# Half the key tiles of an attention stream stored as differences and accumulated onto a used score bank

## The chip, the core and the metric

One core of a Trainium2 chip. The metric is device time in microseconds (us), the median of several executions of one program, lower is better. The engines are TensorE (PE; its weight loads are PEld), VectorE (DVE), ScalarE (ACT), GpSimd (POOL) and the queues that issue DMAs, SyncE's (SP) above all.

## The reference

One layer over 4096 tokens of width 1024 with 16 learned tokens ahead of them (4112 positions). After an RMS norm, one projection feeds two branches:

```python
# Fourier branch: 8 groups of 64 channels, 2-D DFT over positions and channels
fr = jnp.real(jnp.fft.fftn(f, axes=(1, 3), norm='ortho'))
out = jnp.einsum('blgc,gcd->blgd', fr, w_fmix) + b_fmix          # times silu(gate)
# attention branch: 8 query heads, 2 key/value heads of 64, normed and rotated q and k
s = jnp.einsum('bkgqd,bksd->bkgqs', q_blk, k) * (HEAD_DIM ** -0.5)
p = jax.nn.softmax(s, axis=-1)
out = jnp.einsum('bkgqs,bksd->bkgqd', p, v)                      # times silu(gate)
# both: output projection, residual, final RMS norm, the 16 tokens dropped
```

## The kernel before

Everything is computed nearly to float32: an operand is split into a high part in float16 and a low part that holds the rest, and a product is the sum of high x high, low x high and high x low.

**Projection stage** (`phase_a`, to about 700 us). It goes through 33 tiles of 128 positions (tile `NT` = 32 holds the 16 learned tokens) in the order of the list `order`. For each tile TensorE projects to keys and values, queries and two gates (`proj`, in five PSUM banks), VectorE and POOL rotate and norm, `tile_stack` splits queries and keys and `tile_tr` writes them to DRAM (`q_d`, `k_d`); values go to `v_d`. A list of slots (`at`, `deal`) hangs the work of the Fourier branch between the tiles: folds on POOL (`fold_scale`, `fold_lo`), VectorE and ScalarE, and their matmuls (`fproj`).

A key tile is kept as two 128x128 matrices `K[kv][:, 0]` and `K[kv][:, 1]`, written by DMA transposes (`k_load`, `k1_load`). The first has the high part of the keys in rows 0 to 63 and again in 64 to 127; the second has the low part in rows 0 to 63 and the constant 256 in rows 64 to 71. A query block `qA` has high and low parts above each other; `qB` the high part and, in rows 64 to 71, the row maxima times -1/256. So two full matmuls of 512 columns give a score less its bound:

```python
T.matmul(s, K[kv][:, 0, t * P:(t + 1) * P], qa, start=True, stop=False)
T.matmul(s, K[kv][:, 1, t * P:(t + 1) * P], qb, start=False, stop=True)
```

**Stream** (`phase_b`, from about 780 us). 8 query blocks of 512 by 4 pairs of heads make 32 pairs. A pair is 66 steps, 33 key tiles for each of two heads. A step (`step`) has:

- the two score matmuls into one of two banks `s` (pool `pq`);
- `pe`, the exp on ScalarE;
- `rr`, the residual `pe` less its upper half, on POOL or VectorE (VectorE at 16 of the 66);
- five steps later (`LAG = 5`, list `pend`) nine value matmuls into the bank `o` (`pvm`), four query groups of 128 columns. At a head's end ScalarE copies `o` to `tt`, and VectorE and POOL divide and gate.

A bound on each query's scores is needed before its pair. For it 16 **maxima runs** stand in the pair before (list `AT`): a run is two groups (`grp`) of two half-array matmuls, one head in rows 0 to 63 and one in rows 64 to 127 (queries `qP`, copied by DMA), high parts alone, each group into a tile of two banks (pool `pm`, two tiles). VectorE reduces each group over 1024 scores. `red`, `fin` and `put` at steps 61, 63 and 64 turn the maxima into the rows of `qB`; `meta` does the 16 learned tokens. A true maximum is not needed, only a bound that is near enough.

The output projection of the block before (`out_units`, 48 matmuls of 512 columns a pair, at steps 15 to 62 from the fifth pair on) and its norm (`NORM`, `square`, `newton`) are dealt to fixed steps. In the first four pairs (`block0`) the Fourier branch's matmuls stand there instead, two or three a step (`f_step`), with transposes and mixes (`trans`, `mix`) that use `pm` too. Ahead of the first pair its maxima alternate with 11 Fourier matmuls each. After the last pair the last block is projected.

Program order is the order on each engine; the waits come from the tiles.

Of the kernel before, what the change touches and what calls it, by code (L numbers as in the profile page):

```python
# [32 lines left out]
P = 128  # L33
# [5 lines left out]
NT = 32  # L39
# [90 lines left out]
def phase_a(tc, a, pool, mm3, id16, id32, sc):  # L130
# [15 lines left out]
    pos = {t: j for j, t in enumerate(order)}  # L146
    with ExitStack() as st:
# [18 lines left out]
        ksb = [wp.tile([P, 2, 2, 2, HD], F16, name=f"ks{i}") for i in range(3)]  # L166
# [157 lines left out]
        def tile_kv(t):  # L324
# [16 lines left out]
            store(v_d[t, :n], vst[:n])  # L341
# [29 lines left out]

        def tile_stack(t):

            n, qn, ks = xs[t][0], live[t]["t1"], ksb[pos[t] % 3]
            kn = qn[:n, 8 - live[t]["o"]:]
# [4 lines left out]
            S.activation(ks[:n, :, 0, 0], kn, AF.Copy)  # L380
            S.activation(ks[:n, :, 0, 1], kn, AF.Copy)
            V.tensor_tensor(out=ks[:n, :, 1, 0], in0=kn, in1=ks[:n, :, 0, 0], op=ALU.subtract)

        def tile_tr(t):
            n, ks = xs.pop(t)[0], ksb[pos[t] % 3]
            z = live.pop(t)
            store(k_d[t * P:t * P + n], ks[:n].rearrange("p a w b c->p (a w b c)"))
# [220 lines left out]
        def runs(ts):  # L608
            out = [(t, t + 1) for t in ts if t == NT]
            for t in sorted(ts):  # L610
                if t < NT:
                    if out and out[-1][1] == t:
                        out[-1] = (out[-1][0], t + 1)
                    else:
                        out.append((t, t + 1))
            return out

        at(done * 4 + 2 - 3 * 4, ld["k_load"], runs(order[:done]))
        ld["rest"] = runs(order[done:])
# [10 lines left out]
        for t in ksb:  # L630
            G.memset(t, 0.0)
            G.memset(t[:, :, 1, 1, 0:8], 256.0)
# [107 lines left out]
def phase_b(tc, a, pool, mm3, id32, id16, sc):  # L740
# [10 lines left out]
    with ExitStack() as st:  # L751
# [5 lines left out]
        pm = pool(st, "pm", 2, PSUM)  # L757
        pq = pool(st, "pq", 2, PSUM)
        pv = pool(st, "pv", 1, PSUM)
        pp = pool(st, "po", 1, PSUM)  # L760
        K = [ld["kk"][0], bp.tile([P, 2, (NT + 1) * P], F16, name="K1")]
# [3 lines left out]
        qP = [bp.tile([P, 4, QB], F16, name=f"qP{i}") for i in range(2)]  # L765
# [25 lines left out]
        def v_load(i):  # L791
            if i == 3:
# [87 lines left out]
        def trans(u, early):  # L880
# [3 lines left out]
            else:  # L884
                ps = pm.tile([P, 2, 512], F32, tag="m", name="m")[:, 0].rearrange("p (g c)->p g c", c=P)
# [40 lines left out]
        def mix(u, early):  # L926
            n = 64 if seq[u] is LAST else P
            mo = mos[:, 2 * (u % 2):2 * (u % 2) + 2]
            if early:
                t = [pq.tile([P, 512], F32, tag="s", name="s") for _ in range(2)]  # L930
            else:
                t = pm.tile([P, 2, 512], F32, tag="m", name="m")
                t = [t[:, i] for i in range(2)]
# [86 lines left out]

        met, rowt = {}, []

        def max_units(i):
            b, p = pairs[i]
            kv, q, n = p // 2, qP[b % 2], nm[i % 2]
            mx = sm.tile([P, 4, 2, 8], F32, tag="mx", name="mx")

            def grp(s, c):
                t = pm.tile([P, 2, 512], F32, tag="m", name="m")
                for e in range(2):  # L1030
                    rs = slice(64 * e, 64 * e + 64)
                    T.matmul(t[:, e], q[rs, p, s * P:(s + 1) * P], K[kv][rs, 0, c * 512:(c + 1) * 512],  # L1032
                             start=True, stop=True)
                V.tensor_reduce(mx[:, s, :, c], t, axis=AX.X, op=ALU.max)  # L1034

            def meta():
# [4 lines left out]
                t = pm.tile([P, 2, 512], F32, tag="m", name="m")  # L1041
                for x in ps:
                    for e in range(2):
                        rs = slice(64 * e, 64 * e + 64)
                        for s in range(4):
                            o = 64 * x + 16 * s
                            T.matmul(t[:, e, o:o + 16], q[rs, x, s * P:(s + 1) * P], K[x // 2][rs, 0, NTOK:L],
                                     start=x == ps[0] and s == 0, stop=True, skip_group_check=x > ps[0] or s > 0)
                mb = met[b][:, :, ps[0]:ps[-1] + 1]
                V.tensor_reduce(mb, t[:, :, 64 * ps[0]:64 * ps[-1] + 64].rearrange("p e (x s k)->p e x s k", s=4, k=16),  # L1050
                                axis=AX.X, op=ALU.max)
                V.tensor_scalar(out=mb, in0=mb, scalar1=-1.0 / 256.0, scalar2=None, op0=ALU.mult)

            def red():
                m = sm.tile([P, 4, 2], F32, tag="mm", name="mm")
                V.tensor_reduce(m, mx, axis=AX.X, op=ALU.max)
                V.scalar_tensor_tensor(out=n[:, 64:72].rearrange("p (e s)->p e s", s=4),
# [3 lines left out]
            def fin():  # L1061

                t = pm.tile([P, 2, 512], F32, tag="m", name="m")
                T.matmul(t[:, 0, :P], n, id16, start=True, stop=True)
                rowt.append(t)

            def put():
                t = rowt.pop()
                V.tensor_tensor(  # L1069
                    out=qB[b % 2].rearrange("p (q e) (s c)->p e s q c", e=2, c=P)[64:72, :, :, p],  # L1070
                    in0=t[64:72, 0, :P].unsqueeze(1).unsqueeze(1).broadcast_to([8, 2, 4, P]),
                    in1=id32[64:72, 64:72].rearrange("p (e s)->p e s", s=4).unsqueeze(3).broadcast_to([8, 2, 4, P]),
# [503 lines left out]
```

## Time and profile before

| | |
|---|---|
| time, median of 3 executions | 3203.95 us (3200.87 to 3204.02) |
| the profiled execution | 3203.48 us, span 3201.7 us |
| mean granted TensorE clock | 0.995 |
| busy: TensorE / VectorE / POOL / ScalarE | 98% / 74% / 72% / 52% |

The span is the time from the first to the last instruction of the profile. A busy share is that of the time in which at least one instruction of the engine ran. TensorE's matmuls overlap, so that the mean duration of one is longer than the time from its start to the start of the next. A row of the costliest groups reads: line, engine, operation, output and inputs, form and count, then busy us and mean ns of one, then how long the engine stood idle just before these instructions, and what ended most of that.

### The profile page before, as it was taken

How to read it: one execution, taken by the hardware profiler on the slowest of the kernel's cores; microseconds unless marked ns; L12 is line 12 of the kernel's file. 1: busy time of each engine (PE TensorE's matmuls, PEld its weight loads, DVE VectorE, ACT ScalarE, POOL GpSimd, SP SyncE). 2: the span in 40 equal slices, each digit the busy share in tenths (PEclk: the TensorE clock that was granted, in tenths of full speed). 3: DMA queues.
4: the chain of work that ended last, by engine and by line, in shares of the span. 5: the costliest groups of instructions: out<-in, count | busy, mean ns of one | idle time of the engine just before them, and what ended most of it. 6: DMA issues, size and time to landing. Idle time of an engine off the chain costs nothing.

```text
span 3201.7 us, 77151 instructions
## 1 busy us (share of the span) xinstructions
PE 3146.1 (98%) x32291; PEld 1831.4 (57%) x32291; DVE 2373.2 (74%) x3241; ACT 1667.2 (52%) x2965; POOL 2304.3 (72%) x2174
## 2 busy tenths in 40 slices
PE   8999999998999999999999999999999999999998
PEld 4555555545666655555555555555555555555554
DVE  6666566647677778878888778788887887788774
ACT  5433333324555555555555555555555555555563
POOL 5655565536777788877877888887787778888762
PEclk9999999999999999999999999999999999999999
DMA  7444544648422221012111211201120111111112
GB/s 243 146 161 147 152 156 153 182 155 228 131 68 86 78 61 31 28 28 64 28 28 38 54 28 31 58 28 28 38 54 28 35 41 43 31 31 28 28 49 68
DMA packets 238832, 247.67 MB, mean 77 GB/s; under 512 B 134658, under 2 KB 182658, under 8 KB 235538
## 3 DMA queue, kind: packets, MB, share of 16 engines
q1 hardware_dynamic: 224658, 217.57, 23.6%
q10 hardware_dynamic: 13824, 25.17, 2.1%
q8 instruction: 252, 4.13, 0.5%
q14 instruction: 98, 0.80, 0.1%
HBM read 139.59 MB, written 66.38 MB: 64 GB/s over the span
## 4 chain that ended last, share of the span: by engine, by line
PE 74%; DVE 1%; ACT 0%; DMA 0%; issue 0%; POOL 0%; SPq 0%; ACTq 0%; DVEq 0%; POOLq 0%
PE s L1102 14%; PE s L1101 14%; PE o L1122 13%; PE po L1197 9%; PE m L1032 8%; PE o L1129 8%; PE o L1127 2%; PE o L1125 2%; PE pd L849 2%; PE m L1389 1%; DMA acs<-acs_d 0%; ACT pe L1105 0%; POOL rr L1107 0%; DVE rr L1107 0%; DVE thl L893 0%
## 5 line engine op out<-in xcount | busy, mean ns | idle before, releaser
L1107 POOL TENSOR_TENSOR rr<-pe 128x512 f16<-128x512 f32 x1572 | 1709.9, 1105 | 469.9 <-ACT pe L1105 463.4
L1105 ACT ACTIVATE pe<-s 128x512 f32<-128x512 f32 x2112 | 1259.5, 597 | 1016.1 <-PE s L1102 903.2
L1034 DVE TENSOR_REDUCE mx<-m 128x2 f32<-128x1024 f32 x1024 | 1205.9, 1220 | 180.7 <-PE m L1032 179.2
L1129 PE MATMUL o<-VV,rr 128*128 128x65 f16 x8448 | 975.7, 193 | 0.2 <-POOL rr L1107 0.2
L1129 PEld LDWEIGHTS <-rr 128*128 128x128 f16 x8448 | 784.5, 98 | 175.6 <-POOL rr L1107 7.4
L1122 PE MATMUL o<-VV,pe 128*128 128x129 f16 x6336 | 843.3, 222 | 0.8 <-ACT tt L1133 0.8
L1102 PE MATMUL s<-qB,K 128*128 128x512 f16 x2112 | 800.3, 379 | 1.4 <-DVE qB L1069 1.4
L1101 PE MATMUL s<-qA,K 128*128 128x512 f16 x2112 | 799.6, 379 | 0.7 <-ACT pe L1105 0.7
L1122 PEld LDWEIGHTS <-pe 128*128 128x128 bf16 x6336 | 591.1, 97 | 365.1 <-issue 191.0
L1107 DVE TENSOR_TENSOR rr<-pe 128x512 f16<-128x512 f32 x540 | 453.4, 840 | 213.8 <-ACT pe L1105 207.1
L1125 PE MATMUL o<-VV,pe 128*128 128x65 f16 x2112 | 411.5, 195 | 0.0
L1127 PE MATMUL o<-VV,pe 128*128 128x64 f16 x2112 | 410.6, 194 | 0.0
L303 PE MATMUL ps<-wh,xh 128*128 128x512 f16 (+2 forms) x1032 | 352.7, 354 | 9.5 <-ACT xh L291 9.0
L304 PE MATMUL ps<-wl,xh 128*128 128x512 f16 (+2 forms) x1032 | 352.6, 354 | 2.5 <-DVE wl L274 2.5
L1032 PE MATMUL m<-K,qP 64*128 64x512 f16 x2048 | 313.7, 382 | 9.6 <-DMA qP<-qA 6.0
L306 PE MATMUL ps<-wh,xl 128*128 128x512 f16 x768 | 291.6, 380 | 0.0
L1127 PEld LDWEIGHTS <-pe 128*128 128x128 bf16 x2112 | 209.2, 99 | 0.0
L1125 PEld LDWEIGHTS <-pe 128*128 128x128 bf16 x2112 | 206.5, 98 | 0.0
L1102 PEld LDWEIGHTS <-K 128*128 128x128 f16 x2112 | 205.1, 97 | 1.7 <-issue 1.6
L1101 PEld LDWEIGHTS <-K 128*128 128x128 f16 x2112 | 203.4, 96 | 0.9 <-issue 0.4
L1032 PEld LDWEIGHTS <-qP 64*128 64x128 f16 x2048 | 59.7, 94 | 229.2 <-issue 221.3
L1197 PE MATMUL po<-woh,mt 128*128 128x512 f16 x448 | 169.8, 379 | 1.0 <-DVE hh L1202 1.0
(209 smaller groups left out, 3429.2 us busy)
## 6 DMA issues: line engine op xcount, KB each, us to landing
room<-x SPq DMA_DIRECT2D x32, 512.0 KB
xt<-xt SPq DMA_DIRECT2D x32, 512.0 KB
sg<-fx SPq DMA_DIRECT2D x16, 1024.0 KB
xr<-x SPq DMA_DIRECT2D x32, 512.0 KB
out<-yo SPq DMA_DIRECT2D x32, 512.0 KB
ct<-cdo SPq DMA_DIRECT2D x9, 1088.0 KB
fg_d<-g ACTq DMA_DIRECT2D x32, 256.0 KB
ag_d<-g ACTq DMA_DIRECT2D x32, 256.0 KB
```

The costliest lines, as they stand in the source:

```text
L303: T.matmul(o, xh[:, d, :n], wh[:, d, c0:c1], start=d == 0, stop=False)
L1032: T.matmul(t[:, e], q[rs, p, s * P:(s + 1) * P], K[kv][rs, 0, c * 512:(c + 1) * 512], start=True, stop=True)
L1034: V.tensor_reduce(mx[:, s, :, c], t, axis=AX.X, op=ALU.max)
L1101: T.matmul(s, K[kv][:, 0, t * P:(t + 1) * P], qa, start=True, stop=False)
L1102: T.matmul(s, K[kv][:, 1, t * P:(t + 1) * P], qb, start=False, stop=True)
L1105: S.activation(pe, s, AF.Exp, scale=HD ** -0.5)
L1107: eng.tensor_tensor(out=rr, in0=pe, in1=hi, op=ALU.subtract)
L1122: T.matmul(o[:, c0:c0 + 129], hi[:, cs], va, start=t == 0 and s == 0, stop=t == NT, skip_group_check=True)
L1125: T.matmul(o[:, c0:c0 + 65], hi[:, cs], vh, start=False, stop=t == NT, skip_group_check=True)
L1127: T.matmul(o[:, c0:c0 + 64], hi[:, cs], vl, start=False, stop=t == NT, skip_group_check=True)
L1129: T.matmul(o[:, c0:c0 + 65], rr[:, cs], vh, start=False, stop=t == NT, skip_group_check=True)
L1197: T.matmul(d["po"], mts[b, s][i // 4][:, i % 4 + (4 if w == 2 else 0)], wol[i // 4][:, i % 4, cs] if w == 1 else woh[0][:, i, cs], start=j ...
```

## The change

Keys are stored so that of each two neighbours in `order` the first is a base tile and the second holds its difference to the base (`base`), split into high and low after the subtraction, which POOL does. `place` puts four bases and their four differences side by side, so that 8 tiles are loaded as bases in columns 0 to 511 and differences in 512 to 1023; values are stored in the same order. In the second matrix of a base the constant rows move to rows 0 to 7 and the low part to rows 64 to 127; that of a difference has the low part twice. `qB` has its parts the other way round and now serves the maxima of the second head as well, so `qP` goes.

In the stream (order `SEQ`: the learned tokens, then two bases, their two differences, and so on) a base has its two full matmuls as before. A difference has one full matmul, accumulated onto the bank of its base after the exp of the base has read it; the low part is a half-array matmul (`low`). The low parts of two differences stand in the two halves of the array, at the head of a maxima run, every fourth step (`RUNS`).

The maxima of a base and its difference are taken together: a run has four half-array matmuls into four banks, ScalarE takes the relu of the difference's scores, and one VectorE operation adds the base's scores and takes the maximum (`part`). Runs are drawn from a queue that is two ahead (`AHEAD`). Residuals go to VectorE at 42 of 66 steps. The steps of the output matmuls and of `NORM`, `red`, `fin`, `put` move a little, and the tail and the Fourier mixes take single banks. The diff, cut to its core:

```diff
+    base, place = {}, {NT: NT}
+    for i in range(NT // 2):
+        tb, tr = order[1 + 2 * i], order[2 + 2 * i]
+        base[tr] = tb
+        place[tb] = 8 * (i // 4) + i % 4
+        place[tr] = place[tb] + 4
...
         def tile_stack(t):
...
-            S.activation(ks[:n, :, 0, 0], kn, AF.Copy)
-            S.activation(ks[:n, :, 0, 1], kn, AF.Copy)
-            V.tensor_tensor(out=ks[:n, :, 1, 0], in0=kn, in1=ks[:n, :, 0, 0], op=ALU.subtract)
+            if t in base:
+                dk = live[t]["sq"][:, 8:10]
+                G.tensor_tensor(out=dk, in0=kn, in1=keys[base[t]], op=ALU.subtract)
+                kn = dk
+            S.activation(ks[:n, :, 0], kn.unsqueeze(2).broadcast_to([n, 2, 2, HD]), AF.Copy)
+            if t in base:
+                V.tensor_tensor(out=ks[:n, :, 1], in0=kn.unsqueeze(2).broadcast_to([n, 2, 2, HD]), in1=ks[:n, :, 0],
+                                op=ALU.subtract)
+            else:
+                V.tensor_tensor(out=ks[:n, :, 1, 1], in0=kn, in1=ks[:n, :, 0, 1], op=ALU.subtract)
...
-        at(done * 4 + 2 - 3 * 4, ld["k_load"], runs(order[:done]))
-        ld["rest"] = runs(order[done:])
+        at(done * 4 + 2 - 3 * 4, ld["k_load"], [(NT, NT + 1), (0, 24)])
+        ld["rest"] = [(24, NT)]
...
-        pm = pool(st, "pm", 2, PSUM)
+        pm = pool(st, "pm", 4, PSUM)
         pq = pool(st, "pq", 2, PSUM)
...
             for x in part:
-                for e in range(2):
-                    dma(qP[b % 2][64 * e:64 * e + 64, 2 * x:2 * x + 2], q[0:64, 4 * x + e:4 * x + 4:2])
-            for x in part:
-                dma(qB[b % 2][0:64, 4 * x:4 * x + 4], q[0:64, 4 * x:4 * x + 4])
+                for e in (1, 0):
+                    dma(qB[b % 2][64:P, 4 * x + e:4 * x + 4:2], q[0:64, 4 * x + e:4 * x + 4:2])
...
+        SEQ = [NT] + [8 * o + 2 * x + y + z for o in range(4) for x in range(2) for y in (0, 4) for z in range(2)]
...
-            def grp(s, c):
-                t = pm.tile([P, 2, 512], F32, tag="m", name="m")
-                for e in range(2):
-                    rs = slice(64 * e, 64 * e + 64)
-                    T.matmul(t[:, e], q[rs, p, s * P:(s + 1) * P], K[kv][rs, 0, c * 512:(c + 1) * 512],
+            q = [qA[b % 2][0:64], qB[b % 2][64:P]]
+            def grp(s, o):
+                ts = [pm.tile([P, 512], F32, tag="m", name="m") for _ in range(4)]
+                for x in range(4):
+                    e, c0 = x % 2, o * 1024 + (512 if x < 2 else 0)
+                    T.matmul(ts[x], q[e][:, 2 * p + e, s * P:(s + 1) * P], K[kv][64 * e:64 * e + 64, 0, c0:c0 + 512],
                              start=True, stop=True)
-                V.tensor_reduce(mx[:, s, :, c], t, axis=AX.X, op=ALU.max)
+                def part(e):
+                    rl = rp.tile([P, 512], F32, tag=f"rl{e}", name=f"rl{e}")
+                    S.activation(rl, ts[e], AF.Relu)
+                    V.tensor_tensor_reduce(out=rl, in0=ts[2 + e], in1=rl, scale=1.0, scalar=-3.0e38,
+                                           op0=ALU.add, op1=ALU.max, accum_out=mx[:, s, e, o:o + 1])
+                return [lambda: part(0), lambda: part(1)]
...
             def put():
                 t = rowt.pop()
...
+                row = sm.tile([8, P], F16, tag="row", name="row")
+                S.activation(row, t[0:8, :P], AF.Copy)
+                V.tensor_tensor(out=qB[b % 2][0:8, 2 * p:2 * p + 2].rearrange("p h (s c)->p (h s) c", c=P),
+                                in0=row.unsqueeze(1).broadcast_to([8, 8, P]), in1=diag, op=ALU.mult)
...
+            def qk():
+                if n < NT and n % 8 >= 4:
+                    s = d["s"] = banks.pop(n - 4)
+                    T.matmul(s, K[kv][:, 0, cs], qa, start=False, stop=False, skip_group_check=True)
+                else:
+                    s = d["s"] = banks[n] = pq.tile([P, 512], F32, tag="s", name="s")
+                    T.matmul(s, K[kv][:, 0, cs], qa, start=True, stop=False)
+                    T.matmul(s, K[kv][:, 1, cs], qb, start=False, stop=True)
+            def low(x):
+                r = slice(64 * x, 64 * x + 64)
+                T.matmul(d["s"], K[kv][r, 1, cs], (qb if x else qa)[r], start=False, stop=True, skip_group_check=True)
+            def ex(eng):
...
+                S.activation(pe, d["s"], AF.Exp, scale=HD ** -0.5)
...
-        AT = [0, 5, 9, 15, 19, 23, 26, 30, 34, 38, 42, 45, 49, 52, 55, 58]
-        MT, TR, O0, O1 = 60, 12, 15, 39
-        NORM = [9, 13, 17, 21, 28, 32]
+        RUNS = [33 * e + 4 * x for e in range(2) for x in range(1, 9)]
+        AHEAD = 2
+        MT, TR = 60, 11
+        OUT = [4] + list(range(9, 32)) + list(range(37, 61))
+        OUT0 = list(range(16, 40)) + list(range(41, 65))
+        NORM = [7, 11, 15, 19, 23, 28]
...
-            on_dve = {j + 2 for j in AT[:-1]} | {2 * NT + 1}
+            on_dve = {j for j in range(66) if j % 33 == 0 or j % 33 % 4 in (2, 3) or j % 33 % 8 == 4}
...
-            for j, (qk, pvm) in enumerate(stream(i)):
-                qk(V if j in on_dve else G)
+            for j, (qk, half, ex, pvm) in enumerate(units):
+                n = j % 33
+                qk()
+                if n != 4 and j in plan:
+                    plan[j]()
+                if j in RUNS:
+                    end = pend.pop(0)() if n == 4 and pend else None
+                    units[j - 1][1](0)
+                    half(1)
+                    more = draw()
+                    if more:
+                        parts.extend(more())
+                    if n == 4 and j in plan:
+                        plan[j]()
+                    for x in (j - 1, j):
+                        units[x][2](V if x in on_dve else G)
+                        if end:
+                            end()
+                            end = None
+                    if parts:
+                        parts.pop(0)()
+                elif n % 4 != 3:
+                    ex(V if j in on_dve else G)
+                    if parts:
+                        parts.pop(0)()
```

More of the change, by code (lines that the diff above doesn't have):

```diff
@@ L165, in phase_a @@
         dch = wp.tile([P, P], F32, name="dch")
-        ksb = [wp.tile([P, 2, 2, 2, HD], F16, name=f"ks{i}") for i in range(3)]
+        ksb = [wp.tile([P, 2, 2, 2, HD], F16, name=f"ks{i}") for i in range(4)]
         vsb = [wp.tile([P, 2, 129], F16, name=f"vst{i}") for i in range(3)]
@@ L1061, in fin @@
             def fin():
-                t = pm.tile([P, 2, 512], F32, tag="m", name="m")
-                T.matmul(t[:, 0, :P], n, id16, start=True, stop=True)
+                t = pm.tile([P, 512], F32, tag="m", name="m")
+                T.matmul(t[:, :P], n, id16, start=True, stop=True)
                 rowt.append(t)
@@ L1140, in pvm @@
                     G.tensor_tensor(out=dst, in0=dst, in1=rc.unsqueeze(2).broadcast_to([P, 4, HD]), op=ALU.mult)
-            return qk, pvm
+                return end
+            return qk, low, ex, pvm
         pst, mts, mfs = {}, {}, {}
@@ L1281, in phase_b, with draw @@
         put()
+        queue = []
+        def draw():
+            while not queue and len(ends) + 1 < len(pairs):
+                i = len(ends) + 1
+                gs, meta, red, fin, put = max_units(i)
+                queue.extend(gs)
+                ends[i] = (meta, red, fin, put)
+            return queue.pop(0) if queue else None
+        ends = {}
+        parts = []
+        for _ in range(AHEAD):
+            rest = draw()()
+            catch_up()
+            for f in rest:
+                f()
+            f_step(INIT, 1, True)
         assert fcur["i"] >= SPARE
@@ L1301, in phase_b, with flush @@
         pend = []
+        def flush():
+            end = pend.pop(0)()
+            if end:
+                end()
         prev = None
@@ new lines, in phase_b @@
+            plan = {}
+            if halves:
+                plan = dict(zip(OUT if i > 4 else OUT0, halves[0][0] + halves[0][1]))
+            for j, (qk, half, ex, pvm) in enumerate(units):
[14 more added lines that the diff above has]
+                        units[x][2](V if x in on_dve else G)
+                        if end:
+                            end()
+                            end = None
[5 more added lines that the diff above has]
+                        parts.pop(0)()
+                if j == (TR if i > 4 else 12) and b > 0:
+                    low = out_tr(b - 1, p)
+                last = {}
+                if i + 1 < len(pairs):
+                    meta_, red_, fin_, put_ = ends.get(i + 1, (None,) * 4)
+                    last = {60: red_}
+                    if j == MT and meta_:
+                        meta_[0]()
@@ L1357, in phase_b @@
                     load_xr(b, 0)
[L1358 removed]
+                if j == (TR if i > 4 else 12) + 1 and b > 0:
                     low()
@@ L1365, in phase_b @@
                 if len(pend) > LAG:
-                    pend.pop(0)()
+                    flush()
+                if j == 62 and i + 1 < len(pairs):
+                    fin_()
+                    put_()
         b = NQB - 1
@@ L1383, in tail_mm @@
             if part == 0:
-                accs[s] = pm.tile([P, 2, 512], F32, tag="m", name="m")
+                accs[s] = [pm.tile([P, 512], F32, tag="m", name="m") for _ in range(2)]
             for k in range(2):
```

126 lines of the change are left out of this document (48 added, 78 removed).

## The prediction

> **What bounds the kernel now.** I read the page first: busy shares, the chain that ended last, the costliest groups.
>
> ```profile
> span 3201.7 us, 77151 instructions
> PE 3146.1 (98%) x32291; PEld 1831.4 (57%) x32291; DVE 2373.2 (74%) x3241; ACT 1667.2 (52%) x2965; POOL 2304.3 (72%) x2174
> ...
> PE s L1102 14%; PE s L1101 14%; PE o L1122 13%; PE po L1197 9%; PE m L1032 8%; PE o L1129 8%; PE o L1127 2%; PE o L1125 2%; PE pd L849 2%; PE m L1389 1%; DMA acs<-acs_d 0%; ACT pe L1105 0%; POOL rr L1107 0%; DVE rr L1107 0%; DVE thl L893 0%
> ...
> L1107 POOL TENSOR_TENSOR rr<-pe 128x512 f16<-128x512 f32 x1572 | 1709.9, 1105 | 469.9 <-ACT pe L1105 463.4
> L1105 ACT ACTIVATE pe<-s 128x512 f32<-128x512 f32 x2112 | 1259.5, 597 | 1016.1 <-PE s L1102 903.2
> L1034 DVE TENSOR_REDUCE mx<-m 128x2 f32<-128x1024 f32 x1024 | 1205.9, 1220 | 180.7 <-PE m L1032 179.2
> ...
> L1102 PE MATMUL s<-qB,K 128*128 128x512 f16 x2112 | 800.3, 379 | 1.4 <-DVE qB L1069 1.4
> L1101 PE MATMUL s<-qA,K 128*128 128x512 f16 x2112 | 799.6, 379 | 0.7 <-ACT pe L1105 0.7
> L1107 DVE TENSOR_TENSOR rr<-pe 128x512 f16<-128x512 f32 x540 | 453.4, 840 | 213.8 <-ACT pe L1105 207.1
> ...
> L1032 PE MATMUL m<-K,qP 64*128 64x512 f16 x2048 | 313.7, 382 | 9.6 <-DMA qP<-qA 6.0
> ```
>
> TensorE is busy 98% of the span and the chain is nearly all its lines; the two score lines carry 28%. Its idle time ahead of a score matmul is 2.1 us in all. ScalarE waited 903 us for scores, so it follows TensorE. A busy matmul (379 ns) isn't its price, since they overlap; for prices I read the timeline of TensorE where no output matmuls run, a step of the stream and a maxima run:
>
> ```profile
> 2211.48 0.38 PE L1101 MATMUL s<-qA,K 128*128 128x512 f16 x1
> 2211.70 0.38 PE L1102 MATMUL s<-qB,K 128*128 128x512 f16 x1
> 2212.01 0.60 PE L1032 MATMUL m<-K,qP 64*128 64x512 f16 x4
> 2212.54 0.23 PE L1122 MATMUL o<-VV,pe 128*128 128x129 f16 x1
> ...
> 2212.91 0.38 PE L1101 MATMUL s<-qA,K 128*128 128x512 f16 x1
> 2213.13 0.38 PE L1102 MATMUL s<-qB,K 128*128 128x512 f16 x1
> 2213.34 0.22 PE L1122 MATMUL o<-VV,pe 128*128 128x129 f16 x1
> ...
> 2213.70 0.38 PE L1101 MATMUL s<-qA,K 128*128 128x512 f16 x1
> ```
>
> A step takes 0.79 us (2212.91 to 2213.70): two score matmuls of 0.217, then 0.36 of value matmuls. With a run it takes 1.43, so a run costs 0.64. Four half-array maxima lasted 0.60, which is 0.38 + 0.22: they ran two at a time, 0.215 a pair. So 0.43 of the 0.64 is work and 0.21 is the change to half arrays and back: 0.31 from L1102 to the first maximum instead of 0.217, and 0.54 to the value matmuls instead of 0.43.
>
> The length of a pair of heads comes from the one copy that ends each head:
>
> ```profile
> L1133 ACT ACTIVATE tt<-o x64: 538/547/547, 826.4 to 3148.9; 128x452 f32<-128x452 f32 x64
> core 0: us, PE busy (x) PEld busy (x) DVE busy (x) ACT busy (x) POOL busy (x), PEclk, DMA share, GB/s
> ...
> 2202.00:2276.00 74.00, 74.00 (x883) 42.59 (x881) 60.18 (x70) 42.47 (x73) 59.51 (x60) 1.00 0.11 30
> ```
>
> 63 intervals in 2322.5 us: 36.87 a head, 73.7 a pair. TensorE never stops in a late pair, and the clock is full. By the prices above, 66 steps, 16 runs and 48 output matmuls (0.215) are 52.1 + 10.2 + 10.3 = 72.7, so the prices hold.
>
> **The change, part by part.**
>
> *Score matmuls.* Of a head's 33 key tiles, 16 become differences. Such a tile gives up its second full matmul: 32 x 0.217 = 6.94 us a pair off. Their low parts come back as half-array matmuls, two side by side in a run that exists already: 16 x 0.215 = 3.44 on. The 16 runs keep their 64 maxima, and the 0.21 of each is paid before and after. Net 3.50 us a pair. The last pair of heads had no maxima, so there 16 x (0.215 + 0.21) = 6.8 eats the 6.94. So 31 x 3.50 = 108.5 us off the path.
>
> *Maxima on ScalarE and VectorE.* Per pair, 32 reduces of 1024 (1.22 us) become 32 relus and 32 fused adds with maximum over 512. No relu stands in the trace; the nearest rows are ACT reads of a score bank, 597 ns for 512 columns and 547 for 452 (tt), so 0.60, between 0.55 and 0.68 (the gate's silu, L369). The fused operation isn't there either. The nearest with its operands is L1202, which reads a PSUM bank and an SBUF tile; above it stands L1034, over twice the elements:
>
> ```profile
> L1202 DVE SCALAR_TENSOR_TENSOR hh<-po,xr 128x512 f32<-128x512 f32 x56 | 38.7, 691 | 35.4 <-PE po L1197 35.4
> L1107 DVE TENSOR_TENSOR rr<-pe x540: 673/693/1602, 786.6 to 3147.4; 128x512 f16<-128x512 f32 x180
> L1214 ACT ACTIVATE xr<-hh 128x1024 f32<-128x1024 f32 x28 | 29.4, 1049 | 0.0
> L369 ACT ACTIVATE g<-ps,rw 128x512 f32<-128x512 f32 x64 | 43.5, 680 | 111.1 <-PE ps L306 111.1
> ```
>
> I take 0.69, between 0.69 and 1.22. VectorE also takes 42 of 66 residuals instead of 16. Their median is 0.69 and the mean 0.84; I put the excess down to meetings with POOL, busy 80% of the pair shown. POOL keeps 24 x 1.04 + 4.1 = 29 us (about 40%), so half the excess: 0.76. VectorE's other work in that window is 60.2 - 33 x 1.22 - 14.1 (16 residuals) = about 6 us, with the overlaps of its neighbours 7.2. A pair then asks 22.1 + 31.9 + 7.2 = 61.2 us of VectorE, 85% of what I expect a pair to last: covered, as long as the five steps between a residual and its value matmul (some 5 us) take up the bunching.
>
> The Trainium skill, "Vector Engine (DVE) Microarchitecture Reference", section "Points that are easy to get wrong", says of one fused two-source shape that two non-bf16 sources in SBUF halve its rate, no port being left to read the accumulator back. Here one source lies in PSUM, and no run here shows the operation; by the rule the price would be the upper end, the third rival.
>
> *The score banks.* This takes part of the gain back. Two banks serve four tiles: base B0 and B1, then their differences D0 and D1, each onto the bank whose exp must have ended. ScalarE now also has 32 relus a pair. The hand-over in the trace, at the start of the stream, and a step with output work:
>
> ```profile
> 784.96 1.08 ACT L1105 ACTIVATE pe<-s 128x512 f32<-128x512 f32 x2 [0.48 <-PE s L1102]
> ...
> 785.61 0.38 PE L1101 MATMUL s<-qA,K 128*128 128x512 f16 x1 [0.25 <-ACT pe L1105]
> ```
> ```profile
> 2200.67 0.38 PE L1102 MATMUL s<-qB,K 128*128 128x512 f16 x1
> ...
> 2200.89 0.38 PE L1197 MATMUL po<-woh,at 128*128 128x512 f16 x1
> ...
> 2201.09 0.60 ACT L1105 ACTIVATE pe<-s 128x512 f32<-128x512 f32 x1 [0.99 <-PE s L1102]
> ```
>
> An exp begins 0.42 us after its last matmul started; two in a row start 0.48 apart (1.08 - 0.60); TensorE enters a bank 0.05 after its exp (785.56 to 785.61). Four steps without output work: 2 x 0.79 + 2 x 0.577 + 0.855 = 3.59 us of TensorE (the run is 0.64 + 0.215). From their start, exp B0 begins at 0.64, the relu left from the run before at 1.12, exp B1 at 1.60 and ends at 2.20; TensorE wants its bank for D1 at 2.16 and waits 0.09. Exps D0 and D1 and the first relu then run into the next group, where exp B1 is 0.11 later: 0.2 us. With output matmuls a group takes 4.45 us, D1 comes 0.65 later and nothing waits.
>
> Output work is missing at steps 62 to 65, 0 to 8 and 33 to 36 of a pair, and other ScalarE work lies there: the copy of the row of maxima at 62, tt (0.55) between exps D0 and D1 at 4 and 37, the square (1.05) at 7. Following the same schedule: 0.32 at step 65; 0.10, 0.12, 0.17, 0.38 and 0.10 from step 5 to 9; 0.25 from 37 to 41; 1.45 us a pair. 27 pairs have it (the four beside the Fourier work get 2.5 of its matmuls a step, the last has no relus): 39 us back. Its ends: 0, and the 0.2 in all 16 groups as well, another 12 x 0.2 x 27 = 65 us.
>
> *Before the stream.* The first pair's maxima:
>
> ```profile
> 717.00:784.00 67.00, 55.18 (x487) 36.38 (x489) 49.52 (x47) 24.52 (x53) 38.08 (x25) 0.92 0.79 227
> L1034 DVE TENSOR_REDUCE mx<-m 128x2 f32<-128x1024 f32 x32 | 38.0, 1221 | 18.1 <-PE m L1032 18.1
> ```
>
> VectorE drops from 38 to 22 us; TensorE idled 11.8, the most there is to win. I take half, -6; the two groups drawn ahead only move work out of the first pair.
>
> *The projection stage.*
>
> ```profile
> 200.00:700.00 500.00, 496.76 (x2907) 285.31 (x2906) 302.96 (x663) 183.18 (x349) 268.47 (x185) 0.99 0.51 162
> L418 POOL TENSOR_TENSOR sg<-sg,rb 128x1024 f32<-128x1024 f32 (+1 forms) x36 | 79.3, 2223 | 4.9 <-DMA sg<-fx 4.6 <-ACT ks L380 0.3
> L340 POOL TENSOR_TENSOR vst<-vs,vst 128x128 f16<-128x128 f32 (+1 forms) x33 | 22.2, 675 | 5.3 <-ACT vst L339 5.3
> ```
>
> 16 subtractions on POOL (0.68 each by L340) can queue behind a fold of 2.22 us, and ScalarE's key copy waits in order for them, with the gate's silu and the square of the next tile behind it. TensorE has five projection banks of 2.6 to 5.2 us; a ScalarE late by 3 us is covered. 0, at the worst 16 x 2.2 = 35. One key copy fewer (0.29 us) and a doubled low part lie beside it. On SP's queue the key loads become fewer, larger transposes and the query copies four instead of six: 0, as a block's queries are needed three pairs later; at the first block, where the maxima waited 6.0 us for such a copy (L1032 above), it lies within the -6. The row of maxima is written from step 62 with one more ScalarE copy, four steps ahead of its use: 0; without that cover some 1 us a pair.
>
> *Sum.* 3201.7 - 108.5 + 39 - 6, and some 5 us where transposes and mixes of the Fourier part meet the four maxima banks (0 to 12, unpriced in the trace): 3131. The profiled execution took 3203.5, 1.8 over its span and 0.5 below the median of the runs: **3133 us**.
>
> **The rivals.**
>
> 1. The hand-over hides (ScalarE's 1016 us of idle time speak for it, the two banks against): 3133 - 39 = 3094. Chance 0.17.
> 2. It bites in every group, or late residuals do: 3133 + 65 = 3198; from 3165 on, 0.13. For it: ScalarE goes from 42.5 to some 58 us a pair and VectorE to 85%.
> 3. Slower: the fused operation costs 1.22. VectorE then asks 39.0 + 31.9 + 7.2 = 78.1 us against the 73.7 of now and bounds the stream: 31 x 4.4 = +136, 3340. It decides from (73.7 - 31.9 - 7.2) / 32 = 1.08 us on. Against it: L1202's 0.69. 0.08. It is what the skill's rule above gives.
> 4. The change doesn't do what it says: the low parts run one after the other. 16 x 0.217 more a pair cancels the gain: 3133 + 31 x 3.5 = 3242. Against it: four maxima in 0.60. 0.04.
>
> **How the numbers follow.** My forecast, 3110 to 3165, has 0.55, and 0.03 is left for no change. Measured runs spread 0.1% (3200.9 to 3204.0), so 0.2% (6.4 us) is about what can be told. Faster 0.55 + 0.17 + 0.13 = 0.85, the same 0.03, slower 0.12. The range, 3088 to 3198, takes rivals 1 and 2 in and leaves out 3, 4 and no change, 0.15, with the edges 0.2.
>
> **What would show it.** Right: a pair near 71.6 us by the tt copies; TensorE's busy time some 3030 to 3060; a wait of a difference's first matmul for exp of about 40 us in all, at steps 4 to 8 and 65; two low parts starting within a few ns; fused operations near 0.7 and VectorE's residuals near 0.76; no table load between exps and relus. Wrong: that wait spread over all groups, fused operations over 0.9 us (VectorE then over 95% of a pair), low parts 0.217 apart, or value matmuls waiting for residuals.

## The result and the profile after

| | before | after |
|---|---|---|
| time, median | 3203.92 us (4 executions, 3200.87 to 3204.02) | 3185.41 us (4 executions, 3184.41 to 3188.97) |
| span of the profiled execution | 3201.7 us | 3182.6 us |
| mean late pair of heads (ninth to sixty-third copy `tt`, 27 pairs) | 72.73 us | 71.91 us |

The ratio is 0.9947, interval 0.9929 to 0.9964: faster by 18.5 us, where 71 were forecast. The page after, its head and the groups that answer to those shown of before:

```profile
span 3182.6 us, 80710 instructions
PE 3094.5 (97%) x32291; PEld 1814.6 (57%) x32291; DVE 2375.6 (75%) x5079; ACT 2028.8 (64%) x3990; POOL 1450.6 (46%) x1387
...
L1130 ACT ACTIVATE pe<-s 128x512 f32<-128x512 f32 x2112 | 1241.2, 613 | 644.1 <-PE s L1125 605.3
L1132 DVE TENSOR_TENSOR rr<-pe 128x512 f16<-128x512 f32 x1346 | 1007.7, 763 | 330.7 <-ACT pe L1130 312.4
...
L1045 DVE CUSTOM_DVE_ANT_0 rl<-m,rl 128x512 f32<-128x512 f32 x1024 | 702.1, 687 | 159.2 <-ACT rl L1044 146.7
...
L1044 ACT ACTIVATE rl<-m 128x512 f32<-128x512 f32 x1024 | 630.6, 617 | 8.0 <-PE m L1039 7.2
...
L1117 PE MATMUL s<-qA,K 128*128 128x512 f16 x1024 | 387.6, 378 | 10.9 <-ACT pe L1130 8.4
...
L1039 PE MATMUL m<-K,qB 64*128 64x512 f16 x1024 | 310.4, 377 | 15.3 <-DVE mx L1045 10.9
...
L1125 PE MATMUL s<-qB,K 64*128 64x512 f16 x512 | 198.0, 387 | 0.0
```

The durations came out as priced: the fused operation 687 ns (0.69 forecast), VectorE's residual 763 (0.76), the relu 617 (0.60). TensorE's busy time fell by 51.6 us, the span by 19.1. New are its stops: ahead of the maxima for VectorE (`mx`), ahead of a difference's matmul for the exp.

The prices on TensorE held too. Its timeline at two groups with output matmuls:

```profile
2208.78 0.39 PE L1125 MATMUL s<-qA,K 64*128 64x512 f16 x1
2208.78 0.39 PE L1125 MATMUL s<-qB,K 64*128 64x512 f16 x1
...
2209.01 0.38 PE L1039 MATMUL m<-K,qA 64*128 64x512 f16 x1
...
2209.91 0.38 PE L1120 MATMUL s<-qA,K 128*128 128x512 f16 x1
...
2214.36 0.38 PE L1120 MATMUL s<-qA,K 128*128 128x512 f16 x1
```

Two low parts start together, maxima follow 0.23 later, and four steps take 4.45 us (2209.91 to 2214.36), as forecast, without a wait. So the 3.50 us a pair are there; they are lost at other steps.

**Where they went.** The span is divided at five marks, each the start of an instruction in both traces: the last projection matmul, the first score matmul, and the first, ninth and sixty-third copy `tt`, which ends a head. The work drawn ahead of the stream runs from 785.92 to 791.12 us in the timeline of after, 5.2 us.

| stretch | before | after | difference | forecast |
|---|---|---|---|---|
| to the last projection matmul | 708.3 | 713.9 | +5.6 | 0 |
| to the first score matmul | 73.4 | 77.2 | +3.8 | -6 for the maxima, +5.2 for the work drawn ahead |
| first head | 44.7 | 46.9 | +2.2 | |
| next eight heads (Fourier branch) | 328.3 | 318.8 | -9.5 | -14 and -5.2, +5 for the Fourier part |
| next 54 heads, 27 late pairs | 1963.6 | 1941.6 | -22.0 | -55 |
| last head and tail | 83.4 | 84.2 | +0.8 | |

The sum is -19.1. The biggest gap is in the late pairs: 0.82 us won in each instead of 2.05. I took one late pair (from 2201 us) and, at each of its 66 steps, the time to the next step's first score matmul less its price from the prediction's timeline. What is over is a wait, 2.96 us in all:

| steps | over, us | foreseen |
|---|---|---|
| 64, and 2 to 8 | 0.23 + 1.06 | 0.32 + 0.87 |
| 37, 40 | 0.25 | 0.25 |
| 32 | 0.73 | none |
| 61 | 0.40 | none |
| 20 | 0.29 | none |

The hand-over of the score banks is 1.54 in all, where 1.45 was forecast. The other half, 1.42, was not foreseen.

This pair is not a usual one. With the same prices for all 26 whole late pairs (starts of the score matmuls in the trace of after), step 32 loses 0.72 to 0.74 in each. Step 61 loses 0.39 only in the six pairs that take maxima of the 16 learned tokens, and step 20 0.28 to 0.57 in four. Step 62 loses 0.24 in 19 others, where the matmul of `fin` waits for a relu (in the next pair it starts at 2337.74, and the relu ends at 2337.68). In the mean a pair loses 1.45 us to the hand-over, as forecast, and 1.1 at places that were not foreseen, 0.73 of it at step 32. That step in the timeline:

```profile
2229.18 0.69 DVE L1045 CUSTOM_DVE_ANT_0 rl<-m,rl 128x512 f32<-128x512 f32 x1
...
2229.26 0.63 ACT L1044 ACTIVATE rl<-m 128x512 f32<-128x512 f32 x1
...
2229.79 1.81 DVE L1258 SCALAR_TENSOR_TENSOR yo<-hh,rf,fgb 128x1024 f32<-128x1024 f32 x1
...
2231.32 0.38 PE L1039 MATMUL m<-K,qA 64*128 64x512 f16 x1
2231.32 0.38 PE L1039 MATMUL m<-K,qB 64*128 64x512 f16 x1
2231.52 0.68 DVE L1045 CUSTOM_DVE_ANT_0 rl<-m,rl 128x512 f32<-128x512 f32 x1
2231.54 0.38 PE L1039 MATMUL m<-K,qA 64*128 64x512 f16 x1
...
2232.26 0.37 PE L1039 MATMUL m<-K,qB 64*128 64x512 f16 x1 [0.35 <-DVE mx L1045]
```

The second relu of the run at step 28 was done at 2229.89, but VectorE had the block's last scaling (`yo`, `NORM`'s 28) of 1.81 us ahead of the second fused operation. The bank of the fourth maximum comes free only after it: 2232.26 instead of beside 2231.54, 0.72 late, and the step is 0.73 longer. The wait column says only 0.35, since the third maximum is listed as busy for 0.38 of that time. At step 20 the output matmul waits for the DMA that transposes the rows (`at`). Their low part on VectorE ends 16.7 to 17.0 us after the pair's first score matmul in pairs with and without this wait, so VectorE is not what differs. At 61 the maxima after the 16 learned tokens come apart behind `hh` and two reductions, 0.75 together, on VectorE. TensorE is busy 71.20 us of the 72.00 from 2201: the profile shows 0.8 of the 2.96, since a busy matmul (0.38) covers the start of a wait after its 0.217.

### The profile page after: what moved, and what is told of

It reads as the page before. It is cut to its first block, busy times and chain, and to the rows that moved or that the text cites. A ratio compares the mean times of both kernels' runs of the same rounds, so it can differ in the third digit from the quotient of the medians.

```text
span 3182.6 us, 80710 instructions
## 1 busy us (share of the span) xinstructions
PE 3094.5 (97%) x32291; PEld 1814.6 (57%) x32291; DVE 2375.6 (75%) x5079; ACT 2028.8 (64%) x3990; POOL 1450.6 (46%) x1387
## 4 chain that ended last, share of the span: by engine, by line
PE 66%; ACT 5%; DVE 4%; DMA 2%; issue 2%; POOL 1%; SPq 0%; ACTq 0%; DVEq 0%; POOLq 0%
PE o L1147 11%; PE po L1227 8%; PE o L1154 7%; PE s L1120 7%; PE s L1117 7%; PE s L1121 6%; PE m L1039 6%; PE s L1125 5%; ACT pe L1130 3%; PE o L1152 2%; PE o L1150 2%; ACT rl L1044 2%; PE pd L858 1%; DVE yo L1258 1%; PE m L1469 1%
## 5 line engine op out<-in xcount | busy, mean ns | idle before, releaser
L1130 ACT ACTIVATE pe<-s 128x512 f32<-128x512 f32 x2112 | 1241.2, 613 | 644.1 <-PE s L1125 605.3
L1132 POOL TENSOR_TENSOR rr<-pe 128x512 f16<-128x512 f32 x766 | 811.4, 1068 | 1193.9 <-ACT pe L1130 1193.4
L1132 DVE TENSOR_TENSOR rr<-pe 128x512 f16<-128x512 f32 x1346 | 1007.7, 763 | 330.7 <-ACT pe L1130 312.4
L1045 DVE CUSTOM_DVE_ANT_0 rl<-m,rl 128x512 f32<-128x512 f32 x1024 | 702.1, 687 | 159.2 <-ACT rl L1044 146.7
L1044 ACT ACTIVATE rl<-m 128x512 f32<-128x512 f32 x1024 | 630.6, 617 | 8.0 <-PE m L1039 7.2
L1121 PE MATMUL s<-qB,K 128*128 128x512 f16 x1088 | 411.3, 378 | 0.0
L1039 PE MATMUL m<-K,qB 64*128 64x512 f16 x1024 | 310.4, 377 | 15.3 <-DVE mx L1045 10.9
L1039 PE MATMUL m<-K,qA 64*128 64x512 f16 x1024 | 304.9, 377 | 8.0 <-ACT rl L1044 4.1
L1125 PE MATMUL s<-qB,K 64*128 64x512 f16 x512 | 198.0, 387 | 0.0
```

The costliest lines, as they stand in the source:

```text
L1039: T.matmul(ts[x], q[e][:, 2 * p + e, s * P:(s + 1) * P], K[kv][64 * e:64 * e + 64, 0, c0:c0 + 512], start=True, stop=True)
L1044: S.activation(rl, ts[e], AF.Relu)
L1045: V.tensor_tensor_reduce(out=rl, in0=ts[2 + e], in1=rl, scale=1.0, scalar=-3.0e38, op0=ALU.add, op1=ALU.max, accum_out=mx[:, s, e, o:o + 1])
L1121: T.matmul(s, K[kv][:, 1, cs], qb, start=False, stop=True)
L1130: S.activation(pe, d["s"], AF.Exp, scale=HD ** -0.5)
L1132: eng.tensor_tensor(out=rr, in0=pe, in1=hi, op=ALU.subtract)
```

## The experiments

My theory: what the late pairs lose are single places where a bank comes free late, each with its own cause, in VectorE's order (V-type) or in the exps at steps without output matmuls (H-type); freed, they give back what they cost. The rivals: a freed wait turns up at the next step, because an engine behind the banks is the bound; or the pairing itself gains little.

**e1_scale: the scaling one step later.** Changed from after, as all that follow:

```
-        NORM = [7, 11, 15, 19, 23, 28]
+        NORM = [7, 11, 15, 19, 23, 29]
```

> The last part of the output norm (yo, 1.8 us on VectorE) is moved from step 28 of a pair to step 29, behind the second fused operation of the run at 28. Theory M: in the changed kernel yo stands ahead of that operation on VectorE, the bank is free late, and the fourth maximum of the run at 32 waits; 0.72 us in each of 27 pairs, so 3166 to 3170 us and no wait of a maximum for a fused operation at step 32. Rival V: VectorE is too full altogether and the wait only moves to another run: 3180 to 3189.

3176.96 us (ratio to before 0.9921, 0.9907 to 0.9934), between the two ranges; late pairs 71.63. `yo` takes 1.28 us at its new place, so the edit changes its length as well as its order, and the two were not tested apart. The 0.73 at step 32 is gone, and step 37 is at 0.60 instead of 0.16: 0.28 a pair won instead of 0.72, the rest moved five steps on.

**e2_out: the output matmuls spread,** three to a group, so that fewer groups are without one; the block's end at step 65.

```
-        OUT = [4] + list(range(9, 32)) + list(range(37, 61))
+        OUT = [j for j in range(1, 16) if j % 4 and j not in (11, 15)] + [18, 19] + list(range(21, 33)) + [j for j in range(34, 66) if (j - 33) % 4]
-                if j == (62 if i > 4 else 65) and b > 0:
+                if j == 65 and b > 0:
```

> The 48 output matmuls of a pair are spread so that every group of four steps has two to four of them, three as a rule (none were at steps 0 to 3, 5 to 8, 33 to 36 and 61 to 65). Theory H: the waits for the score banks are there because TensorE has too little other work between two bases and the second difference; with it they go: 1.05 us at steps 64 to 9 and 0.24 at 37 to 41, and the 0.27 of the wait for a transpose at step 20, 1.4 to 1.5 us in 27 pairs, so 3145 to 3150 us. Rival R: ScalarE is late by its load as a whole (89% of a pair), or the residuals are, and the waits spread over the groups with the matmuls: 3175 to 3187. The wait at step 32 (theory M) stays in either.

3176.04 us (0.9917, 0.9903 to 0.993), in the rival's range; late pairs 71.56. Still, the hand-over waits at 64 and 2 to 8 fell from 1.29 to 0.57, but 0.42 at step 16, 0.37 at 37 and 0.20 at 57 stand in their place.

**e3_both: both edits.**

> Both moves. If H and M hold and are independent: 3185 - 38 - 17 = 3130 us, a late pair near 69.6 us. If the one wait hides behind the other: 3145 to 3165.

3161.28 us (0.987, 0.9856 to 0.9883); late pairs 71.08. The gain is 24.1 us, more than the two together (8.4 + 9.4), so they do not compete, but it is short of the 55 that independent parts would give and lies in the range of the second expectation. With the output matmuls spread, moving `yo` alone is worth 14.8 us (3176.04 to 3161.28). TensorE's waits from 1121 to 3080 us (total, times, longest), after and here:

```profile
PE m L1039 <- DVE mx L1045: 9.3, 26, 0.4
PE s L1117 <- ACT pe L1130: 7.5, 31, 0.3
PE s L1120 <- ACT pe L1130: 1.9, 7, 0.4
```
```profile
PE s L1120 <- ACT pe L1130: 20.2, 65, 0.7
PE s L1117 <- ACT pe L1130: 0.9, 4, 0.3
```

The waits of the maxima are gone from the list, that of a new base's bank is there: steps 4 and 37 have a copy `tt` on ScalarE and no output matmul now. At 16 a maxima wait is left that the list does not show: the low part of the output rows (`low`, 1.28 us) stands ahead of a fused operation on VectorE, and the fourth maximum starts at 2271.49 instead of beside the third at 2271.06.

**e5_dk: the keys' subtraction on VectorE** instead of POOL, for the +5.6 of the projection.

```
-                G.tensor_tensor(out=dk, in0=kn, in1=keys[base[t]], op=ALU.subtract)
+                V.tensor_tensor(out=dk, in0=kn, in1=keys[base[t]], op=ALU.subtract)
```

> The difference of two key tiles is subtracted on VectorE instead of POOL. The projection stage ended 5.6 us later than before the change. Theory P: ScalarE's key copy waits in order behind a subtraction that queues on POOL (22.4 us in 11 waits), and what is late behind it delays TensorE: then 3180 to 3182 us and the last projection matmul 3 to 5 us earlier. Rival: the doubled low part on VectorE, or the start, costs it: 3184 to 3188, and no earlier.

3185.89 us (0.9948, 0.9936 to 0.9961): no gain. The last projection matmul is at 714.1. ScalarE's wait for it in the first 720 us, after and then here:

```profile
ACT ks L396 <- POOL sq L394: 19.3, 10, 3.9
```
```profile
ACT ks L396 <- DVE sq L394: 32.0, 15, 4.9
```

The key copy waits for the subtraction on whichever engine does it.

**e9_ks: the copy and low part of a difference one tile later,** with the tile's store, so that ScalarE does not stand for the subtraction.

```
-                dk = live[t]["sq"][:, 8:10]
+                dk = live[t]["t2"][:, 8:10]
...
+            if t in base:
+                return
             S.activation(ks[:n, :, 0], kn.unsqueeze(2).broadcast_to([n, 2, 2, HD]), AF.Copy)
...
             z = live.pop(t)
+            if t in base:
+                kn = z["t2"][:, 8:10].unsqueeze(2).broadcast_to([n, 2, 2, HD])
+                S.activation(ks[:n, :, 0], kn, AF.Copy)
+                V.tensor_tensor(out=ks[:n, :, 1], in0=kn, in1=ks[:n, :, 0], op=ALU.subtract)
             store(k_d[
```

> The key copy on ScalarE and the low part on VectorE of a difference tile are issued with the tile's store, one tile later, so that nothing on ScalarE stands behind the subtraction on POOL. Theory Q (the copy blocks ScalarE's queue; the squares behind it are late and the first transpose of the row norms waits 6.5 instead of 3.4 us): the projection stage ends 3 to 5 us earlier, 3180 to 3182 us. Rival (the start or VectorE's doubled low part): 3184 to 3187.

3180.01 us (0.9926, 0.9914 to 0.9939), 5.4 less. The last projection matmul in the query of its line (minimum/median/maximum ns, first to last start), before, after and here, and what TensorE waits for here from 700 to 833 us:

```profile
L306 PE MATMUL ps<-wh,xl x768: 377/379/634, 22.2 to 708.3; 128*128 128x512 f16 x192
```
```profile
L312 PE MATMUL ps<-wh,xl x768: 377/379/634, 21.4 to 713.9; 128*128 128x512 f16 x192
```
```profile
L312 PE MATMUL ps<-wh,xl x768: 377/379/634, 20.8 to 707.0; 128*128 128x512 f16 x192
```
```profile
PE m L1041 <- DMA qA<-q_d: 5.7, 1, 5.7
PE pd L860 <- DMA acs<-acs_d: 4.2, 1, 4.2
PE m L1041 <- ACT rl L1046: 4.0, 2, 3.7
```

The projection ends 6.9 earlier, the first score matmul 4.9 (786.2 instead of 791.1): the first maxima now wait for the queries' load. The eight other traces that subtract the keys at the old place on POOL, that of after among them, end the projection between 712.6 and 715.8, e11_best with this edit at 709.8, so the traces' spread of some 3 us does not make this gain.

**e7_full: no pairing.** The low part of a difference is a full matmul with `qA`, and the half-array low parts go.

```
                     T.matmul(s, K[kv][:, 0, cs], qa, start=False, stop=False, skip_group_check=True)
+                    T.matmul(s, K[kv][:, 1, cs], qa, start=False, stop=True, skip_group_check=True)
...
-                    units[j - 1][1](0)
-                    half(1)
```

> One part of the change undone: the low part of a difference is a full matmul of its own, right behind the first one (against the block with the queries' high and low parts), and no half-array pair stands in the runs. Theory W (the saving on TensorE is real, and what is lost are waits): 32 x 0.217 - 16 x 0.215 = 3.5 us more work in each of 31 pairs, 109 us, of which the waits for score banks give back up to 1.3 us a pair as TensorE comes later: 3260 to 3294 us. Rival: the pairing saves little by itself, as changing to half arrays or accumulating onto a used bank costs it: below 3225.

3207.35 us (1.0011, 1.0002 to 1.002), 21.9 slower than after: this is the rival's side. A late pair takes 72.72, that of before 72.73, the same TensorE work by price, and the wait for a bank stands once:

```profile
PE m L1039 <- DVE mx L1045: 0.3, 1, 0.3
```

So the pairing's 3.50 us are not small: full matmuls in their place hide the waits that the steps of after lose, 2.56 a pair in the mean. With shorter steps, ScalarE and VectorE, who free the banks, show.

**e8_relu2: each relu twice** (one execution).

```
                     S.activation(rl, ts[e], AF.Relu)
+                    S.activation(rl, ts[e], AF.Relu)
```

> Each relu is done twice (0.48 us more on ScalarE, 32 times a pair; the result is the same). Theory H (hand-over of the two score banks through ScalarE's queue): in the schedule by hand exp B1 comes 0.96 us later in a group; groups with output matmuls then wait 0.5, those without 1.3: some 11 us in 27 pairs, less beside the Fourier work: 3400 to 3500 us. Rival (ScalarE has time to spare, the waits come from VectorE): below 3225.

3618.61 us, above both ranges: each group with output matmuls loses some 0.8 us at one step (11, 15, 19 and so on), where theory H had 0.5. A late pair takes 86.28, 14.4 more, though ScalarE was busy in only 52.4 us of the 72.0 after. ScalarE and the score matmuls in one group:

```profile
2510.69 0.60 ACT L1045 ACTIVATE rl<-m 128x512 f32<-128x512 f32 x1
...
2511.18 0.59 ACT L1131 ACTIVATE pe<-s 128x512 f32<-128x512 f32 x1
...
2511.66 0.60 ACT L1044 ACTIVATE rl<-m 128x512 f32<-128x512 f32 x1
2511.83 0.38 PE L1118 MATMUL s<-qA,K 128*128 128x512 f16 x1
...
2512.30 0.60 ACT L1045 ACTIVATE rl<-m 128x512 f32<-128x512 f32 x1
2512.79 0.59 ACT L1131 ACTIVATE pe<-s 128x512 f32<-128x512 f32 x1
...
2513.43 0.38 PE L1118 MATMUL s<-qA,K 128*128 128x512 f16 x1 [0.66 <-ACT pe L1131]
```

Two relus stand between two exps: the exps are 1.61 apart (2511.18 to 2512.79), and the second difference's matmul starts 0.05 after the end of its base's exp (2513.38). An average load tells nothing of this: ScalarE has little slack inside a group.

**e6_weak: e3_both with the weak steps filled.** Output matmuls at 4 and 37, `low` and the low part of `mf` one step later (the edits to `NORM` and to the block's end as in e3_both).

```
+        OUT = [1, 2, 3, 4, 5, 6, 7, 9, 10, 13, 14, 18] + list(range(22, 41)) + [42, 43, 44, 46, 47, 48, 50, 51, 52, 54, 55, 56, 58, 59, 62, 63, 64]
-                if j == (TR if i > 4 else 12) + 1 and b > 0:
+                if j == 13 and b > 0:
-                        ready = dict(zip((52, 53, 55), mf_parts(*divmod(i - 3, 4))))
+                        ready = dict(zip((52, 54, 55), mf_parts(*divmod(i - 3, 4))))
```

> Both moves, and three more: the low half of the block's attention output (1.3 us on VectorE, step 12) goes to step 13 and that of the Fourier output (step 53) to step 54, each behind the second fused operation of the run before; and steps 4 and 37 get their output matmul back, the matmuls on that transpose begin at step 22. Theory M+H (single late instructions, each with its place): the waits left in a pair of e3, 0.37 and 0.38 at steps 4 and 37, 0.42 at 16, 0.21 at 57, shrink to 0.15, 0.15, 0 and 0: 1.0 us in 27 pairs, 3161 - 27 = 3134 us. Rival V (VectorE and ScalarE are full, waits move to the next run): 3150 to 3162.

3161.45 us (0.9865, 0.9851 to 0.9878): not faster than e3_both, as the rival had it. But the waits have not crept along; one new one holds them all. TensorE's waits from 1121 to 3080 us, and step 34 in the timeline:

```profile
PE po L1227 <- DVE hh L1232: 19.5, 28, 0.7
PE s L1120 <- ACT pe L1130: 3.5, 13, 0.4
```
```profile
2219.45 0.38 PE L1227 MATMUL po<-woh,at 128*128 128x512 f16 x1
...
2219.98 0.69 DVE L1045 CUSTOM_DVE_ANT_0 rl<-m,rl 128x512 f32<-128x512 f32 x1 [0.28 <-ACT rl L1044]
...
2220.59 0.69 DVE L1232 SCALAR_TENSOR_TENSOR hh<-po,xr 128x512 f32<-128x512 f32 x1
...
2221.34 0.38 PE L1227 MATMUL po<-woh,mt 128*128 128x512 f16 x1 [0.72 <-DVE hh L1232]
```

The 24th output matmul now stands at step 33 and the 25th, the first of the second half, at 34. Between them VectorE must read the one bank `po` out (`hh`), and a fused operation was ahead of it.

**e10_gap: one free step there.** The 25th goes to step 35, and one more goes into 57 (here against e6_weak, the list cut).

```
-        OUT = [...] + list(range(22, 41)) + [..., 54, 55, 56, 58, 59, 62, 63, 64]
+        OUT = [...] + list(range(22, 34)) + list(range(35, 41)) + [..., 54, 55, 56, 57, 58, 59, 62, 63, 64]
```

> Order e6_weak again, with one thing changed: the second head's first output matmul goes one group later (step 35 instead of 34) and one output matmul goes into step 57. In the trace of e6_weak TensorE waits 19.5 us in 28 places (0.7 each) for the read-out of the output bank on VectorE, all at step 34, directly behind the last output matmul of the first head at step 33. Theory M (that one place took back the whole gain of the order): the wait goes or falls to under 0.2, late pairs from 70.8-70.9 to 70.0-70.2 us, 27 to 28 pairs, time 3139 to 3147. Rival V (a wait removed always turns up at the next group, the engines behind the banks are the bound): late pairs stay at 70.7-70.9, time 3157 to 3163, with a new wait of 0.5 or more at some other step.

3138.99 us (0.9796, 0.978 to 0.9813), 22.5 below e6_weak. Late pairs 70.26. That wait is gone and no other came:

```profile
PE s L1120 <- ACT pe L1130: 4.7, 18, 0.4
PE s L1117 <- ACT pe L1130: 1.1, 5, 0.3
```

**e11_best: e10_gap with e9_ks.**

> e10_gap with the moved key copy and low part of the differences from e9_ks. The two parts lie in different stages (projection against stream), so both theories expect e10_gap minus 4 to 6 us: 3134 to 3142 by M, 3152 to 3158 by V. Were it equal to e10_gap, the 5 us of e9_ks would have been given back at the start of the stream.

3134.88 us (0.9787, 0.9772 to 0.9802): 67.8 us or 2.1% below the median of before in the same set of runs (3202.67), and 50.5 below after. It is the fastest version; 4.1 below e10_gap, so the two parts add.

The waits of one late pair by step, from the timelines of six orders, beside the mean length of the 27:

| steps | after | e1_scale | e2_out | e3_both | e6_weak | e10_gap |
|---|---|---|---|---|---|---|
| 64, 2 to 8 | 1.29 | 1.28 | 0.57 | 0.55 | 0.33 | 0.35 |
| 16 to 20 | 0.29 | 0.23 | 0.42 | 0.42 | 0.08 | 0.08 |
| 32 | 0.73 | 0 | 0.52 | 0 | 0 | 0 |
| 34, 35 | 0 | 0.08 | 0 | 0 | 0.87 | 0.08 |
| 37, 40 | 0.25 | 0.60 | 0.46 | 0.47 | 0.26 | 0.25 |
| 57, 61 | 0.40 | 0.39 | 0.20 | 0.21 | 0 | 0 |
| sum in this pair | 2.96 | 2.58 | 2.17 | 1.65 | 1.54 | 0.76 |
| mean of 26 pairs | 2.56 | 2.26 | 2.12 | 1.61 | 1.53 | 0.75 |
| mean late pair | 71.91 | 71.63 | 71.56 | 71.08 | 71.04 | 70.26 |

The last row but one takes, over the 26 whole late pairs, every step whose mean lies more than 0.06 over its price, but for step 60, where the learned tokens' matmuls of every fourth pair add 0.14 to the mean. Length less that mean lies between 69.3 and 69.5 in all six, where the prices give 72.7 - 3.50 = 69.2, and 69.3 with the 0.14. So TensorE's saving was there in each, and the order of small work decides what is seen of it.

## Why the prediction was right or wrong

- *Score matmuls, -108.5 us*: right as a price on TensorE (groups of 4.45 us, low parts together; 69.3 to 69.5 a pair without its waits under all six orders). In the late pairs it is 27 x 3.50 = 94.5.
- *Score banks, +39 us*: right in size and nearly in place: 1.45 a pair in the mean, as forecast (1.54 in the pair read), and the groups with output matmuls do not wait. e2_out and e10_gap showed that it hangs on the missing output matmuls, e8_relu2 that ScalarE is what frees the banks.
- *Maxima on ScalarE and VectorE, "covered"*: here the prediction failed. The prices were right (0.69, 0.76, 0.60), and the upper end of 1.22 for the fused operation, with it the third rival, did not come. On the halved rate of the Trainium skill ("Vector Engine (DVE) Microarchitecture Reference", "Points that are easy to get wrong"), which speaks of two sources in SBUF: with one of them in a PSUM bank this trace shows none, 687 ns for 512 columns. The share was right too (59.25 of 72.0 us, 82%, where 85% was forecast). What was wrong was to judge cover by it, and to look for the bunching at the residuals: "covered, as long as the five steps between a residual and its value matmul (some 5 us) take up the bunching". What came late was the bank of a maximum. VectorE does its work in program order, and its single long operations (1.81, 1.28) and its read-outs stand ahead of a fused operation that frees a maxima bank. At step 32 that cost 0.73 us in every late pair, 20 us in 27 (how much of it is the length of `yo` stands in the last section), and with step 61 (VectorE), 62 (a relu) and 20 (a DMA) 1.1 a pair in the mean, 30 us. e1_scale, and e3_both against e2_out, showed the cause at step 32. Against the forecast's 55 us for the late pairs, 22 came; the missing 33 are 1.23 a pair: this 1.1, and 0.1 that the prices leave open. The rival that named "late residuals" had the size and not the place: the profile lists no value matmul that waits for one.
- *First pair's maxima, -6*: wrong. VectorE's work did fall, but TensorE had waited for it 1.7 us only; half of the 11.8 us of idle time that I halved was a query copy's 6.0. What it waits for between the projections and the first copy `tt` (700 to 826 us before, 700 to 838 after):

```profile
PE m L1032 <- DMA qP<-qA: 6.0, 1, 6.0
...
PE m L1032 <- DVE mx L1034: 1.7, 2, 1.1
PE pd L849 <- DMA acs<-acs_d: 1.6, 1, 1.6
```
```profile
PE pd L858 <- DMA acs<-acs_d: 4.8, 1, 4.8
PE m L1039 <- ACT rl L1044: 4.4, 2, 4.1
PE m L1039 <- DVE fgu L930: 3.9, 1, 3.9
...
PE m L1039 <- DMA qB<-qA: 1.5, 1, 1.5
```

  The copy's wait shrank by 4.5, and a relu, a DMA and a fold on VectorE took its place.
- *Projection stage, 0*: wrong by +5.6, the chain I had named as the worst case (0 to 35): the key copy behind the subtraction. e5_dk showed that the engine does not matter, e9_ks that the order does.
- *The four pairs beside the Fourier part*: 9.5 us won, of which 5.2 only moved ahead of the stream. TensorE's waits there rose from 5.5 to 7.3 us; the rest of the gap was not tested and stays open. The last pair lost 1.2 instead of nothing.
- *The forecast itself*: 3133 was 52 us too low, and the time fell into the second rival's stretch (3165 to 3198), though its mechanism, a wait in all groups, did not occur. Two signs that I had named for a right forecast failed with it: TensorE's busy time is 3094.5 us, not 3030 to 3060, and the wait of a difference's matmul for the exp is listed with 8.4 us, not 40. The step lengths show the hand-over all the same (1.45 a pair), as a matmul that costs 0.217 is listed as busy for 0.38. That e11_best, at 3134.88, lands near 3133 is luck: its order also takes away some 24 of the 39 us that the forecast counts as a loss (in the order of e10_gap the hand-over costs 0.55 a pair).

## What to carry to other kernels

When a saving on the bounding engine shortens its steps, price the engines that free its buffers within one step and in their order, not by their share of the span: a single 1.8 us operation ahead of another one in VectorE's order cost half as much as all hand-overs of the score banks. Measure step lengths against their price, since busy time hides waits. And when a freed wait seems to move on, look which single instruction holds the new one before you conclude that an engine is the bound: one free step between the last matmul into a bank and the first into it again was worth 22 us.

## What the hardware showed that I had not expected

- The fused operation is followed by a separate read of the accumulator on VectorE of 0.08 to 0.09 us, one for each of the 1024 (84.2 us in all); the prediction had not counted these.
- The same scaling of 1024 columns (`yo`) took 1.81 us at step 28 and 1.28 at step 29 (medians 1816 and 1281 ns of 28). What differs is which of two operations began first. In the kernel after, a residual on POOL had begun 0.30 us ahead of `yo` in 26 of 28 cases (2229.48 against 2229.79 in the timeline at step 28): these `yo` took 1.81, the residual its usual 1.04. In the kernel before, the residual began 0.38 us or more after `yo` in 27 of 28 cases: there `yo` took 1.28, and the residual 1.73 to 1.80. Of these two, the one that began second is the one that is longer. So of the 0.72 us at step 32 some 0.5 (an estimate, 1.81 less 1.28) comes from the residual that POOL had begun. The query of the line of `yo` (minimum/median/maximum ns), before and after:

```profile
L1228 DVE SCALAR_TENSOR_TENSOR yo<-hh,rf,fgb x28: 1277/1280/1285, 1222.5 to 3151.8; 128x1024 f32<-128x1024 f32 x28
```
```profile
L1258 DVE SCALAR_TENSOR_TENSOR yo<-hh,rf,fgb x28: 1273/1816/1818, 1221.9 to 3133.1; 128x1024 f32<-128x1024 f32 x28
```

- The wait column understates a late matmul: at step 32 it says 0.35 us where the fourth maximum started 0.72 late and the step lost 0.73.
